# Three 256-column matmuls per weight tile on one accumulator, in place of a 512-column and a 256-column one on two halves that are added later

## The chip, the core and the metric

The kernel runs on one core of a Trainium2 chip. The metric is the device time of one execution in microseconds (us), the median of several runs. The engines that matter here are the tensor engine (PE; its weight loads are shown apart, as PEld), the vector engine (DVE), the scalar engine (ACT) and the queue that issues the loads of the weights (SP).

## What is computed

One decoder layer in float32 for 256 tokens and 2048 features: a norm; in parallel a recurrent branch (RG-LRU) and sliding-window attention; each branch is projected, gated by a sigmoid, and summed; then an output projection, norms, and an MLP with squared ReLU of 8192 features. Cut to what matters:

```python
h = rmsnorm(x, norm_mix_pre)
xr, yr, q, k, v, g_rnn, g_attn = jnp.split(h @ w_in, IN_OFFSETS, axis=-1)
xr = rg_lru(causal_depthwise_conv(xr, conv_w, conv_b), positions, w_rg_a, b_rg_a, w_rg_x, b_rg_x, lru_lambda)
y_rnn = xr * jax.nn.gelu(yr)
y_att = sliding_window_sink_attention(rope(q, positions), rope(k, positions), v, sinks)
mix = sigmoid(g_rnn) * (y_rnn @ w_rnn_proj) + sigmoid(g_attn) * (y_att @ w_attn_proj)
x = x + rmsnorm(mix @ w_out, norm_mix_post)
u = jnp.square(jax.nn.relu(rmsnorm(x, norm_mlp_pre) @ w_mlp_up))
x = x + rmsnorm(u @ w_mlp_down, norm_mlp_post)
```

## The kernel before

**The split.** Each float32 product of a projection is made of three products of reduced-precision parts. An activation x is kept as x_hi + x_lo, a weight w as w_hi + w_lo, and x·w is taken as w_hi·x_hi + w_lo·x_hi + w_hi·x_lo. Activations lie transposed in SBUF as [128 features, k tile, hi/lo, 256 tokens], so that the hi and the lo half of one k tile lie side by side, 512 columns in all. The class `Stream` loads the weights in halves of 128 × 1024 (SP queue, L67) and splits each half on the spot: ACT writes `whi` (L78), DVE writes `wlo` (L79), up to six halves ahead of their use.

**Two kinds of projection.** In `b_step` (L208 to L212) the activations are the stationary operand and the weights stream by in 512-column matmuls; keys, queries, the output projection and the second half of the MLP are made so. In `a_pair` (L179 to L198) a 128 × 128 tile of weights is stationary and the activations stream by. One call of `a_pair` makes two blocks of 128 features for the 256 tokens: 2 blocks × 16 k tiles = 32 weight tiles, in four halves of 8. It has 80 calls: 8 for the gates of the attention's projection, 16 for the two inputs of the recurrent branch (`conv` and `gelu`), 8 for the attention's projection, 8 for the gates of the recurrent branch's projection (`g_rnn`), 8 for that projection itself, and 32 for the first half of the MLP. That is 80 × 32 = 2560 weight tiles.

**One weight tile of `a_pair`.** `whi` is loaded, and one 512-column matmul (L193, `both`) passes x_hi and x_lo behind it, onto both halves of a PSUM bank; `wlo` is loaded, and one 256-column matmul (L192, for the first k tile L195) passes x_hi onto the second half of the same bank. So the bank holds w_hi·x_hi in its first half and the two small products in its second. At the end ACT copies the second halves of both blocks to SBUF (L197) and DVE adds the first halves to them (L198); the code that uses the result reads that SBUF tile.

**PSUM.** It has eight banks. A result of `a_pair` takes two of them; the pool `psa` has two such slots, and after the attention a third (`psa2`) joins them. The gates of the recurrence (`gates`, L610 to L657) have two banks of their own, `psg`. In the output projection and the MLP, `psb2` takes the four banks that `psg` and `psa2` had held.

**The gates of the recurrence.** `gates` has 256-column products of its own: for each of its weight tiles it issues `whi` with x_hi (L624), `whi` with x_lo (L625) and `wlo` with x_hi (L626), all three onto the same 256 columns of one bank, 24 matmuls in a row for each half of weights.

**What sets the order.** Each engine works through its instructions in a fixed order that the framework's scheduler chose when the program was built; an instruction that must wait holds up those behind it on its engine. Attention and the residual are generators whose stages `pump` places between the halves of the products, and some parts are pinned or given priority by hand.

Of the kernel before, what the change touches and what calls it, by code (L numbers as in the profile page):

```python
# [20 lines left out]
P = 128  # L21
# [13 lines left out]
def two_pi_parts():  # L35
    """2*pi in parts of 6 bits each, whose products with integers of up to 18 bits are exact."""
    parts, lsb, rest = [], 2.0 ** -3, TWO_PI
    for _ in range(7):
        c = float(np.floor(rest / lsb) * lsb)
        parts.append(c)  # L40
        rest -= c
        lsb *= 2.0 ** -6
    return parts


class Stream:
    """Weights in the order in which they are used: loads run ahead, and each half of a chunk is
    split into its two float32r parts ahead of the products."""
# [58 lines left out]
def layer(tc, x, pos_t, pos_row, inv_freq, vecs, sinks, gains, w_kv, w_q, w_xy, w_rg, w_g, w_rp, w_ap, w_out,  # L107
# [8 lines left out]
    psa = enter(tc.tile_pool(name="psa", bufs=2, space=bass.MemoryType.PSUM))  # L116
    pairs = [psa, psa]
# [3 lines left out]
    # ---- the weights, in the order of their use  # L121
# [32 lines left out]

    def units(name):
        return [unit(f"{name}{i}") for i in range(4)]
# [6 lines left out]
    def pump(n=1):  # L163
        """one more stage of the work that goes on beside the products"""
        for _ in range(n):
            while waiting:
                try:
                    next(waiting[0])
                    break
                except StopIteration:  # L170
                    waiting.pop(0)

    def pair(name):
        """two banks"""
        pool = pairs[0]
        pairs.append(pairs.pop(0))
        return pool.tile([P, 2, 2, S], F32, tag="pair" + pool.name, name=name)

    def a_pair(acts, out):  # L179
        """out [128 features, 2, 256 tokens] = (two column blocks of weights).T @ acts; both parts of  # L180
        the acts pass behind one load of the weights' high part"""
        ps = pair("ps")
        for f in range(2):
            both = ps[:, f].rearrange("p a b -> p (a b)")
            for half in range(2):
                hi, lo = ws.half()
                for k in range(8):
                    kt = half * 8 + k
                    a = acts[kt // 4][:, kt % 4]
                    c = slice(k * P, k * P + P)  # L190
                    if kt:
                        mm(ps[:, f, 1, :], lo[:, c], a[:, 0, :], start=False, stop=False)  # L192
                    mm(both, hi[:, c], a.rearrange("p a b -> p (a b)"), start=kt == 0, stop=kt == KT - 1)  # L193
# [3 lines left out]
        nc.scalar.copy(out, ps[:, :, 1, :])  # L197
        nc.vector.tensor_tensor(out, ps[:, :, 0, :], out, ALU.add)  # L198
# [15 lines left out]
    def b_pass512(acts, name):  # L214
        """[256 tokens, 512 columns], one bank per token block"""
# [12 lines left out]
    def transpose_split(nat, dst, tb, q, ps):  # L228
        """a quarter of nat [128 tokens, 2048 features] -> dst[q] [128 features, k tile, hi/lo, tokens]"""
# [10 lines left out]
    # ---- phase A: everything up to the merged mixers  # L240
# [37 lines left out]
    def rms(tb, k):  # L278
        """1 / sqrt(mean + eps) from the four partial sums of squares"""
# [7 lines left out]
    # ---- first norm, a token block at a time, and the keys' and values' products behind it  # L287
# [4 lines left out]
    for q in range(4):  # L292
        if q % 2 == 0:
            room = pair("gain_b")
        gain_b.append(room[:, q % 2].rearrange("p a b -> p (a b)"))
# [97 lines left out]
    # ---- rotary tables  # L393
# [25 lines left out]
    def rope(ps, tb, heads, dsts):  # L419
        """ps [128 tokens, heads * 64] -> every dst [128, heads, 64], rotated"""  # L420
# [13 lines left out]
    # ---- keys and values  # L434
# [18 lines left out]
    def attention(g, banks):  # L453
        """one group of eight heads, in stages"""
# [123 lines left out]
    # ---- recurrent branch, two blocks of 256 channels at a time  # L578
# [5 lines left out]
    def conv(n, xc):  # L584
        p3 = wide(t2("px"))
        a_pair(hT, p3)
# [13 lines left out]
    def gelu(n, th):  # L600
        py = t2("py")
        a_pair(hT, wide(py))
# [63 lines left out]
    def attn_proj(p):  # L666
        pp = t2("pp")
        a_pair(yatt, wide(pp))
        m = m1[p // 2][:, 2 * (p % 2) : 2 * (p % 2) + 2, :]
        nc.vector.scalar_tensor_tensor(m, m, 1.0, wide(pp), ALU.add, ALU.mult)  # L670
# [15 lines left out]
    # ---- the recurrent branch's projection, gated, and the merge  # L686
    def g_rnn():
        g = t2("g2")
        a_pair(hT, wide(g))
        nc.scalar.activation(g, g, AF.Tanh, scale=0.5)  # L690
        return g
# [5 lines left out]
    for p in range(8):  # L697
        pp = t2("pp")
        a_pair(yrnn, wide(pp))
# [11 lines left out]
    # ---- phase B: output projection, norms, MLP  # L711
    ctx1.close()
    pairs[:] = [psa]
# [14 lines left out]
    def b_pass1024(acts, n_kt, name, finish, n_held=HELD):  # L728
        """[256 tokens, 1024 columns]; the first token block is finished ahead of the second"""
# [17 lines left out]
    # with x1 = x + r1 * og and h2 = r2 * x1 * g2: h2 / r2 = x * g2 + r1 * (og * g2)  # L747
# [12 lines left out]
    def finish(n, tb, banks):  # L760
# [6 lines left out]
        if n == 0 and tb == 0:  # L767
            # brings the table of Sqrt in ahead of its first use
            nc.scalar.activation(st[:, 31:32], sq[:, 1, 0, 0:1], AF.Sqrt)
        if n == 1:  # L770
            if tb == 1:
                # keeps the clock of the tensor engine up over the norms
                warm = pair("warm")[:, 0, 0, 0:P]
# [6 lines left out]
            for q in range(4):  # L780
                if q % 2 == 0:
                    room = pair("ptr")
                transpose_split(h2[tb], h2T, tb, q, room[:, q % 2].rearrange("p a b -> p (a b)"))
# [19 lines left out]
    def residual():  # L803
        """x1 and r2, beside the first products of the MLP"""
# [35 lines left out]
    for f in range(2):  # L840
        uT = [unit(f"uT{f}{i}") for i in range(8)]
        def evacuate(p, u):
            nc.vector.scalar_tensor_tensor(wide(u), wide(u), 0.0, r2.unsqueeze(1).to_broadcast([P, 2, S]), ALU.max,
# [7 lines left out]
        for p in range(16):  # L851
            u = u2("u")
            a_pair(h2T, wide(u))
            full.append((p, u))
# [33 lines left out]
def lay_out(inp):  # L888
    """The arrays as the program reads them: only moved, never computed on."""
# [18 lines left out]
    # [gate, block, k, j] -> [pair of blocks, 128, block, gate, k tile, j]  # L908
# [40 lines left out]
```

## Time and profile before

| | before |
|---|---|
| measured, us | 1571.42, 1572.79, 1573.88 (median 1572.79) |
| the profiled execution: its span from first to last instruction, us (no other time of this execution is given) | 1571.5 |
| granted TensorE clock, mean | 0.997 |
| weight tiles in `a_pair` | 2560 |
| all matmuls, each with a weight load of its own | 8126 in the trace |
| DVE sums (L198) / ACT copies (L197) after `a_pair` | 80 / 80, 0.69 us / 0.58 us each |

A row of a group in the profile reads: line, engine, operation, output<-inputs by the program's names, shapes, count | busy us, mean ns of one | idle time of the engine ahead of them and who ended it. A matmul's duration runs from its start to the end of its pipeline, so neighbouring matmuls overlap in the records; what a matmul costs is the distance from its start to the next one's start. A window row reads: from:to in us, its length, the busy time with the count of instructions that touch the window, the granted clock, the share of the DMA engines' time and GB/s.

### The profile page before, as it was taken

To read this page: it belongs to the slowest core of one execution; us is meant where nothing else is said; L and a number is where in the kernel's file an instruction comes from. 1 tells how busy PE (TensorE), PEld (TensorE's weight loads), DVE (VectorE), ACT (ScalarE), POOL (GpSimd) and SP (SyncE) were. 2 spreads that over 40 slices of the span, in tenths; PEclk is the share of its full clock that TensorE was granted. 3 is DMA by queue.
4 is the path that set the end of the run, shared out by engine and by line. 5 is a ranking of instruction groups with operands and counts; after the bars stand their busy time and mean duration, and the time that the engine had idled before them with its cause. 6 is when DMAs were issued, how large, how long until landed. Compare 5 with 4: busy or idle time off the path is not lost.

```text
span 1571.5 us, 20784 instructions
## 1 busy us (share of the span) xinstructions
PE 1550.0 (99%) x8126; PEld 1306.0 (83%) x8126; DVE 975.5 (62%) x1164; ACT 804.0 (51%) x1118; POOL 1.7 (0%) x9
## 2 busy tenths in 40 slices
PE   8999999999999999999999999999999999999997
PEld 6887777788888888888787888888888888888886
DVE  6666666857758867555656756554444656554544
ACT  5545545646556775444354645444434555543432
POOL 0000000000000000000000000000000000000000
PEclk9999999999999999999999999999999999999999
DMA  6554344354655456555863555555555555555552
GB/s 247 189 169 148 128 157 149 127 186 162 209 181 194 162 187 207 183 189 185 301 212 115 200 191 181 192 190 192 193 193 187 188 190 185 189 190 196 190 197 96
DMA packets 79876, 287.85 MB, mean 183 GB/s; under 512 B 9249, under 2 KB 9505, under 8 KB 79137
## 3 DMA queue, kind: packets, MB, share of 16 engines
q1 hardware_dynamic: 79200, 285.48, 53.5%
q8 instruction: 63, 1.03, 0.2%
q10 hardware_dynamic: 578, 1.06, 0.2%
q14 instruction: 35, 0.29, 0.1%
HBM read 284.40 MB, written 2.10 MB: 182 GB/s over the span
## 4 chain that ended last, share of the span: by engine, by line
PE 95%; ACT 1%; DVE 1%; DMA 1%; issue 1%; SPq 0%; DVEq 0%
PE ps L193 38%; PE ps L192 18%; PE d L210 7%; PE d L208 7%; PE d L212 7%; PE o L208 2%; PE q L208 2%; PE o L210 2%; PE o L212 2%; PE q L210 2%; PE q L212 2%; PE sc L484 1%; PE ps L195 1%; PE po L524 1%; PE pt L516 1%
## 5 line engine op out<-in xcount | busy, mean ns | idle before, releaser
L79 DVE TENSOR_TENSOR wlo<-wraw,whi 128x1024 fp32r<-128x1024 f32 x528 | 642.7, 1223 | 430.1 <-ACT whi L78 429.1
L78 ACT CAST whi<-wraw 128x1024 fp32r<-128x1024 f32 x528 | 552.7, 1051 | 526.2 <-PE ps L193 193.9
L193 PE MATMUL ps<-hT,whi 128*128 128x512 f32 x1024 | 361.4, 398 | 0.0
L193 PE MATMUL ps<-h2T,whi 128*128 128x512 f32 x1024 | 359.0, 400 | 0.5 <-DVE h2T L237 0.5
L192 PE MATMUL ps<-hT,wlo 128*128 128x256 f32 x960 | 271.1, 282 | 0.0
L192 PE MATMUL ps<-h2T,wlo 128*128 128x256 f32 x960 | 270.7, 282 | 0.0
L193 PEld LDWEIGHTS ps<-h2T,whi 128*128 128x128 f32 x1024 | 189.4, 189 | 43.0 <-DVE h2T L237 0.9
L193 PEld LDWEIGHTS ps<-hT,whi 128*128 128x128 f32 x1024 | 189.8, 188 | 41.1 <-issue 0.7
L192 PEld LDWEIGHTS ps<-hT,wlo 128*128 128x128 f32 x960 | 181.2, 189 | 5.6 <-issue 3.1
L192 PEld LDWEIGHTS ps<-h2T,wlo 128*128 128x128 f32 x960 | 182.3, 190 | 2.6
L212 PE MATMUL d<-whi,uT 128*128 128x512 f32 x512 | 163.3, 389 | 0.0
L208 PE MATMUL d<-whi,uT 128*128 128x512 f32 x512 | 163.3, 390 | 0.0
L210 PE MATMUL d<-wlo,uT 128*128 128x512 f32 x512 | 163.3, 389 | 0.0
L208 PEld LDWEIGHTS d<-whi,uT 128*128 128x128 f32 x512 | 96.1, 188 | 20.1 <-ACT acc L870 0.3
L212 PEld LDWEIGHTS d<-whi,uT 128*128 128x128 f32 x512 | 96.1, 188 | 20.1
L210 PEld LDWEIGHTS d<-wlo,uT 128*128 128x128 f32 x512 | 96.1, 188 | 19.9
L193 PE MATMUL ps<-yrnn,whi 128*128 128x512 f32 x256 | 90.3, 398 | 0.0
L193 PE MATMUL ps<-yatt,whi 128*128 128x512 f32 x256 | 89.6, 399 | 0.0
L192 PE MATMUL ps<-yrnn,wlo 128*128 128x256 f32 x240 | 67.6, 282 | 0.7 <-ACT yrnn L656 0.7
L192 PE MATMUL ps<-yatt,wlo 128*128 128x256 f32 x240 | 67.5, 281 | 0.0
L193 PEld LDWEIGHTS ps<-yrnn,whi 128*128 128x128 f32 x256 | 47.6, 188 | 10.4
L193 PEld LDWEIGHTS ps<-yatt,whi 128*128 128x128 f32 x256 | 47.2, 188 | 10.5
(207 smaller groups left out, 1530.4 us busy)
## 6 DMA issues: line engine op xcount, KB each, us to landing
wraw<-in_w_up SPq DMA_DIRECT2D x128, 512.0 KB, 3.9
wraw<-in_w_dn SPq DMA_DIRECT2D x128, 512.0 KB, 4.0
wraw<-in_w_g SPq DMA_DIRECT2D x64, 512.0 KB, 4.5
wraw<-in_w_xy SPq DMA_DIRECT2D x64, 512.0 KB, 4.2
wraw<-in_w_q SPq DMA_DIRECT2D x32, 512.0 KB, 3.7
wraw<-in_w_ap SPq DMA_DIRECT2D x32, 512.0 KB, 4.5
wraw<-in_w_rp SPq DMA_DIRECT2D x32, 512.0 KB, 4.2
wraw<-in_w_out SPq DMA_DIRECT2D x32, 512.0 KB, 5.0
```

What stands on the lines that cost most here:

```text
L78: self.pin(self.nc.scalar.copy(hi, src))
L79: self.pin(self.nc.vector.tensor_tensor(lo, src, hi.bitcast(F32), ALU.subtract))
L192: mm(ps[:, f, 1, :], lo[:, c], a[:, 0, :], start=False, stop=False)
L193: mm(both, hi[:, c], a.rearrange("p a b -> p (a b)"), start=kt == 0, stop=kt == KT - 1)
L195: mm(ps[:, f, 1, :], lo[:, c], a[:, 0, :], start=False, stop=False)
L208: mm(banks[tb][n], a[:, 0, t], hi[:, n * 512 : n * 512 + 512], start=first, stop=False)
L210: mm(banks[tb][n], a[:, 0, t], lo[:, n * 512 : n * 512 + 512], start=False, stop=False)
L212: mm(banks[tb][n], a[:, 1, t], hi[:, n * 512 : n * 512 + 512], start=False, stop=last)
L484: mm(ps[:, i * w : i * w + w], qT[r0 : r0 + HD, h, tb * P : tb * P + P], kT[r0 : r0 + HD, g, 0:w], start=True, stop=True)
L516: nc.tensor.transpose(ps[:, h * P : h * P + P], s3[:, h % per, kb * P : kb * P + P], ident)
L524: mm(po[par * HD : par * HD + HD, :], v_sb[:, kb, g * HD : g * HD + HD], pT[par, kb], start=kb == 0, stop=kb == nk - 1)
```

## The change

`a_pair` issues three 256-column matmuls per weight tile: w_hi with x_hi, w_hi with x_lo, w_lo with x_hi, all onto the same 256 columns. Its result is half a bank per block, one bank in all, and is complete without an addition. The copy (L197) and the sum (L198) go, and the code that uses the result reads PSUM itself. `psa` has four slots of one bank; `psa2` goes; `psg` has four banks where it had two.

```diff
-    psa = enter(tc.tile_pool(name="psa", bufs=2, space=bass.MemoryType.PSUM))
-    pairs = [psa, psa]
+    psa = enter(tc.tile_pool(name="psa", bufs=4, space=bass.MemoryType.PSUM))
...
     def pair(name):
-        """two banks"""
-        pool = pairs[0]
-        pairs.append(pairs.pop(0))
-        return pool.tile([P, 2, 2, S], F32, tag="pair" + pool.name, name=name)
-
-    def a_pair(acts, out):
+        return psa.tile([P, 2, S], F32, tag="pair", name=name)
+
+    def a_pair(acts):
         ps = pair("ps")
         for f in range(2):
-            both = ps[:, f].rearrange("p a b -> p (a b)")
             for half in range(2):
                 hi, lo = ws.half()
                 for k in range(8):
                     kt = half * 8 + k
                     a = acts[kt // 4][:, kt % 4]
                     c = slice(k * P, k * P + P)
-                    if kt:
-                        mm(ps[:, f, 1, :], lo[:, c], a[:, 0, :], start=False, stop=False)
-                    mm(both, hi[:, c], a.rearrange("p a b -> p (a b)"), start=kt == 0, stop=kt == KT - 1)
-                    if kt == 0:
-                        mm(ps[:, f, 1, :], lo[:, c], a[:, 0, :], start=False, stop=False)
+                    mm(ps[:, f, :], hi[:, c], a[:, 0, :], start=kt == 0, stop=False)
+                    mm(ps[:, f, :], hi[:, c], a[:, 1, :], start=False, stop=False)
+                    mm(ps[:, f, :], lo[:, c], a[:, 0, :], start=False, stop=kt == KT - 1)
                 pump()
-        nc.scalar.copy(out, ps[:, :, 1, :])
-        nc.vector.tensor_tensor(out, ps[:, :, 0, :], out, ALU.add)
+        return ps
...
-            a_pair(hT, m)
-            nc.scalar.activation(m, m, AF.Tanh, scale=0.5)
+            nc.scalar.activation(m, a_pair(hT), AF.Tanh, scale=0.5)
...
-            psg = ctx1.enter_context(tc.tile_pool(name="psg", bufs=2, space=bass.MemoryType.PSUM))
-            pairs.append(ctx1.enter_context(tc.tile_pool(name="psa2", bufs=1, space=bass.MemoryType.PSUM)))
+            psg = ctx1.enter_context(tc.tile_pool(name="psg", bufs=4, space=bass.MemoryType.PSUM))
...
-        def evacuate(p, u):
-            nc.vector.scalar_tensor_tensor(wide(u), wide(u), 0.0, r2.unsqueeze(1).to_broadcast([P, 2, S]), ALU.max,
+        def evacuate(p, ps):
+            u = u2("u")
+            nc.vector.scalar_tensor_tensor(wide(u), ps, 0.0, r2.unsqueeze(1).to_broadcast([P, 2, S]), ALU.max,
                                            ALU.mult)
```

The other callers (`conv`, `gelu`, `attn_proj`, `g_rnn` and the merge) change in the same way: the tile that the copy and the sum had filled goes, and its reader takes the accumulator.

How the instructions stand on the tensor engine, at three places. Names: `h2T`, `yrnn` and `hT` are split activations, `ps` the accumulator, `o` the output projection's, `ptr` a bank for transposes.

First, the first weight tiles of the MLP's first half. Before:

```order
L193 MATMUL ps<-h2T_6748,whi_7263 128x512
L195 MATMUL ps<-h2T_6748,wlo_7264 128x256
L192 MATMUL ps<-h2T_6748,wlo_7264 128x256
L193 MATMUL ps<-h2T_6748,whi_7263 128x512
L192 MATMUL ps<-h2T_6748,wlo_7264 128x256
```

And with the change:

```order
L190 MATMUL ps<-h2T_8154,whi_8669 128x256
L191 MATMUL ps<-h2T_8154,whi_8669 128x256
L192 MATMUL ps<-h2T_8154,wlo_8670 128x256
L190 MATMUL ps<-h2T_8154,whi_8669 128x256
L191 MATMUL ps<-h2T_8154,whi_8669 128x256
```

Two instructions of different width have become three of one width; the accumulator's columns are the same for all three.

Second, the first call of `a_pair` on the recurrent branch's output, where it comes to the last two blocks (`yrnn_5278`, and with the change `yrnn_6243`; each has four k tiles, of which the last two come from the last block). Before:

```order
L193 MATMUL ps<-yrnn_5278,whi_5293 128x512
L192 MATMUL ps<-yrnn_5278,wlo_5294 128x256
L193 MATMUL ps<-hT_138,whi_5359 128x512
L195 MATMUL ps<-hT_138,wlo_5360 128x256
L192 MATMUL ps<-hT_138,wlo_5360 128x256
L193 MATMUL ps<-hT_138,whi_5359 128x512
L192 MATMUL ps<-hT_138,wlo_5360 128x256
L193 MATMUL ps<-yrnn_5278,whi_5293 128x512
```

And with the change:

```order
L190 MATMUL ps<-yrnn_6243,whi_6258 128x256
L191 MATMUL ps<-yrnn_6243,whi_6258 128x256
L192 MATMUL ps<-yrnn_6243,wlo_6259 128x256
L190 MATMUL ps<-yrnn_3760,whi_6288 128x256
L191 MATMUL ps<-yrnn_3760,whi_6288 128x256
```

Before, five matmuls of a later call stand between the two matmuls of the third of those four k tiles; now the call runs through without them. Ahead of this call, with the change, stand the 48 matmuls of the last gates in one row and then the 96 of one call of `a_pair`.

Third, the end of the output projection, where the first token block is transposed for the MLP while the second block's products still run. Before:

```order
L208 MATMUL o_7064<-whi_7191,mixT_5387 128x512
L233 MATMUL ptr<-ident,h_6738 128x128 x4
L210 MATMUL o_7064<-wlo_7192,mixT_5387 128x512
L212 MATMUL o_7064<-whi_7191,mixT_5387 128x512
L208 MATMUL o_7064<-whi_7209,mixT_5387 128x512
L210 MATMUL o_7064<-wlo_7210,mixT_5387 128x512
L233 MATMUL ptr<-ident,h_6738 128x128 x4
L212 MATMUL o_7064<-whi_7209,mixT_5387 128x512
```

And with the change:

```order
L204 MATMUL o_8470<-whi_8597,mixT_6382 128x512
L229 MATMUL ptr<-ident,h_8144 128x128 x4
L206 MATMUL o_8470<-wlo_8598,mixT_6382 128x512
L229 MATMUL ptr<-ident,h_8144 128x128 x4
L208 MATMUL o_8470<-whi_8597,mixT_6382 128x512
L229 MATMUL ptr<-ident,h_8144 128x128 x8
```

The groups of four transposes have moved closer together: one matmul stands between them where there were three or four, and the last group, which had stood behind the second block's products, now stands ahead of most of them.

More of the change, by code (lines that the diff above doesn't have):

```diff
@@ L292, in layer @@
     for q in range(4):
-        if q % 2 == 0:
-            room = pair("gain_b")
-        gain_b.append(room[:, q % 2].rearrange("p a b -> p (a b)"))
+        gain_b.append(narrow(pair("gain_b")))
         mm(gain_b[q], ones, gain[:, quarter(q)], start=True, stop=True)
@@ L584, in conv @@
     def conv(n, xc):
-        p3 = wide(t2("px"))
-        a_pair(hT, p3)
+        p3 = a_pair(hT)
         x3 = wide(xc)
@@ L600, in gelu @@
     def gelu(n, th):
-        py = t2("py")
-        a_pair(hT, wide(py))
+        py = narrow(a_pair(hT))
         u = t2("u")
@@ L666, in attn_proj @@
     def attn_proj(p):
-        pp = t2("pp")
-        a_pair(yatt, wide(pp))
+        pp = a_pair(yatt)
         m = m1[p // 2][:, 2 * (p % 2) : 2 * (p % 2) + 2, :]
-        nc.vector.scalar_tensor_tensor(m, m, 1.0, wide(pp), ALU.add, ALU.mult)
+        nc.vector.scalar_tensor_tensor(m, m, 1.0, pp, ALU.add, ALU.mult)
     for m in range(4):
@@ L688, in g_rnn @@
         g = t2("g2")
-        a_pair(hT, wide(g))
-        nc.scalar.activation(g, g, AF.Tanh, scale=0.5)
+        nc.scalar.activation(g, narrow(a_pair(hT)), AF.Tanh, scale=0.5)
         return g
@@ L697, in layer @@
     for p in range(8):
-        pp = t2("pp")
-        a_pair(yrnn, wide(pp))
+        pp = narrow(a_pair(yrnn))
         g = ahead.pop(0)
@@ L712, in layer @@
     ctx1.close()
-    pairs[:] = [psa]
     ctx2 = ExitStack()
@@ L771, in finish @@
             if tb == 1:
-                warm = pair("warm")[:, 0, 0, 0:P]
+                warm = pair("warm")[:, 0, 0:P]
                 for i in range(WARM_NORM):
@@ L780, in finish @@
             for q in range(4):
-                if q % 2 == 0:
-                    room = pair("ptr")
-                transpose_split(h2[tb], h2T, tb, q, room[:, q % 2].rearrange("p a b -> p (a b)"))
+                transpose_split(h2[tb], h2T, tb, q, narrow(pair("ptr")))
         for i in range(2):
@@ L851, in layer @@
         for p in range(16):
-            u = u2("u")
-            a_pair(h2T, wide(u))
-            full.append((p, u))
+            full.append((p, a_pair(h2T)))
             if f == 0 and p == R2_AT:
```

2 lines of the change are left out of this document (added).

## Prediction

> **What bounds the kernel now.** I read the page's busy times first, then the chain that ended last.
>
> ```profile
> span 1571.5 us, 20784 instructions
> PE 1550.0 (99%) x8126; PEld 1306.0 (83%) x8126; DVE 975.5 (62%) x1164; ACT 804.0 (51%) x1118; POOL 1.7 (0%) x9
> PE 95%; ACT 1%; DVE 1%; DMA 1%; issue 1%; SPq 0%; DVEq 0%
> ```
>
> The tensor engine is busy for 99% of the span and makes up 95% of the chain. Work spared on DVE or ACT cannot show in the time unless the tensor engine waits for it; what counts is the distance from one matmul's start to the next one's. The groups of the tensor engine, shapes kept apart, say how often the changed piece runs:
>
> ```profile
> L193 PE MATMUL ps<-hT,whi 128*128 128x512 f32 x1024 | 361.4, 398 | 0.0
> L193 PE MATMUL ps<-h2T,whi 128*128 128x512 f32 x1024 | 359.0, 400 | 0.5 <-DVE h2T L237 0.5
> L193 PE MATMUL ps<-yrnn,whi 128*128 128x512 f32 x256 | 90.3, 398 | 0.0
> L193 PE MATMUL ps<-yatt,whi 128*128 128x512 f32 x256 | 89.6, 399 | 0.0
> ```
>
> One such matmul per weight tile: 1024 + 1024 + 256 + 256 = 2560 tiles, with hardly any idle time ahead of them. So each nanosecond per tile is 2.56 us. The mean durations are no price, since neighbours overlap; the price comes from windows of the tensor engine that begin and end at starts of matmuls:
>
> ```profile
> core 0: us, PE busy (x), PEclk, DMA share, GB/s
> 512.93:515.66 2.73, 2.73 (x26) 1.00 0.57 197
> ...
> 575.21:577.95 2.74, 2.74 (x26) 1.00 0.58 190
> 578.25:581.10 2.85, 2.85 (x26) 1.00 0.54 180
> 1033.31:1207.62 174.31, 174.31 (x770) 1.00 0.55 187
> 1207.62:1388.31 180.69, 180.69 (x1025) 1.00 0.57 192
> ```
>
> The last row is the first half of the MLP in its second round: 16 calls of `a_pair`, 16 x 32 = 512 weight tiles, 1024 matmuls (a count in a row takes in those that reach into the window). The row above it is `b_step`, 768 matmuls of 512 columns. The first row is one half of weights in `gates`: 24 matmuls of 256 columns, **the very pattern that the change brings**: the same weights twice, then the low part, all three onto the same 256 columns. The timeline shows it beside one tile of `a_pair`:
>
> ```profile
> 1300.08 0.28 PE L192 MATMUL ps<-h2T,wlo 128*128 128x256 f32 x1
> 1300.19 0.40 PE L193 MATMUL ps<-h2T,whi 128*128 128x512 f32 x1
> 1300.43 0.28 PE L192 MATMUL ps<-h2T,wlo 128*128 128x256 f32 x1
> ```
>
> ```profile
> 513.28 0.28 PE L624 MATMUL pg<-xs,whi 128*128 128x256 f32 x1
> 513.39 0.28 PE L625 MATMUL pg<-xs,whi 128*128 128x256 f32 x1
> 513.50 0.28 PE L626 MATMUL pg<-xs,wlo 128*128 128x256 f32 x1
> 513.62 0.28 PE L624 MATMUL pg<-xs,whi 128*128 128x256 f32 x1
> ```
>
> 0.35 us per tile there, 0.34 us here.
>
> **The change, part by part.** *The stream of matmuls.* Before: 180.69 us / 512 = 352.9 ns per tile. With the change: 2.73 us / 24 = 113.8 ns per matmul, times three 341.3 ns (the second `gates` row gives 2.74 / 24, so 342.5). The tile passes 768 columns either way. Where all are of one width the price goes by the column: 174.31 us / 768 = 227.0 ns for 512, twice the 113.5 of a 256. So the 12 ns that `a_pair` pays on top look like the price of alternating widths, and go with it. Saved: 352.9 − 341.3 = 11.6 ns x 2560 = **29.7 us**. The 2560 additional weight loads are within this price, since each `gates` matmul has a load of its own too; what this term rests on is that a pattern seen in runs of 24 and 48 holds for thousands.
>
> Here a rule of the Trainium skill speaks against the change: TensorE: Matmul & The Clock Gate, section Back-to-back issue gap, gives a warm matmul its columns at 2.4 GHz and 2.5 ns on top, whatever the width. By it one matmul more costs 2.5 ns x 2560 = 6.4 us, an estimate from that page, and the sum would end above the time before. The trace disagrees: 113.5 and 227.0 ns are one to two, which leaves no room for such a part.
>
> *Copies and sums.* 80 ACT copies (L197) and 80 DVE sums (L198) go, of 0.58 and 0.69 us each; 32 of them are
>
> ```profile
> L197 ACT COPY u<-ps 128x512 f32<-128x512 f32 x32 | 18.7, 584 | 53.5 <-PE ps L193 53.5
> L198 DVE TENSOR_TENSOR u<-ps,u 128x512 f32<-128x512 f32 x32 | 22.1, 691 | 34.2 <-ACT u L197 34.2
> ```
>
> They lie beside the products, and where nobody waits that is worth nothing. The waits list of the tensor engine names where somebody does:
>
> ```profile
> PE ptr L233 <- DVE h L779: 1.5, 2, 1.2
> PE o L208 <- DVE pp L198: 1.4, 1, 1.4
> ...
> PE ps L192 <- ACT yrnn L656: 0.7, 1, 0.7
> ```
>
> The second row is the start of the output projection: `psb2` takes the banks of `psa2`, and the last sum still reads them. With the change its banks come from `psg`, done 170 us earlier. **1.4 us saved**; next in line are weights that are split far ahead, so nothing replaces it.
>
> *Four banks for `gates`.* The view of line L624 has under idle time:
>
> ```profile
>   ACT room L629: 1.0, 5
> ```
>
> The gates wait for one of their two banks. With four, each call has a bank for each of its four results. **1.0 us saved.**
>
> *The order at the last recurrent block.* Before, products of `hT` fill the time until `yrnn` of the last block is split; with the change fewer stand there. The split was late already:
>
> ```profile
> 597.88 0.39 PE L192 MATMUL ps<-yrnn,wlo 128*128 128x256 f32 x1 [0.72 <-ACT yrnn L656]
> 598.23 0.68 DVE L657 TENSOR_TENSOR yrnn<-xct,yrnn 128x512 fp32r<-128x512 f32 x1
> ```
>
> The gates end at 581.10 (window row above), the low part is there at 598.91, 17.8 us later. With the change the tensor engine comes to it after 96 matmuls and 14 tiles: 96 x 113.8 ns + 14 x 341.3 ns = 15.7 us. It waits for up to 2.1 us in place of 0.7. With four banks the second run of 24 need not start 0.30 us after the first one's end (577.95 to 578.25 in the window rows), so the chain may start that much earlier; I take a wait of 1.7: **1.0 us lost** (between 0.7 gained, with no wait left, and 1.4 lost).
>
> *The transposes at the norms* stand closer together. Four transposes wait for a DVE step of 0.69 us (four in 2.74 us); with one matmul of 0.23 us between, up to some 0.3 us each may be lost, against a last group that no longer stands behind the products. The wait there is 1.5 us in all (first row of the list), so I take 0, between 1 us lost and 1 us gained.
>
> ```profile
> 836.68 2.74 DVE L779 SCALAR_TENSOR_TENSOR h<-h,st,xg 128x512 f32<-128x512 f32 x4
> ```
>
> *Accumulators held longer.* Their readers now hold PSUM itself. With four slots a result has three calls' time, 3 x 32 x 341.3 ns = 32.8 us, until its slot is wanted. The longest hold is at the start of the MLP, where three results wait for `r2`; its matmuls stand at the end of the third call:
>
> ```profile
> 886.13 0.60 PE L833 MATMUL pr<-dg,ones 128*128 128x128 f32 x4
> ```
>
> The fifth call wants the first slot some 11 us after that, and the first reader is one DVE step. Cost 0; if a hold broke this cover, each microsecond would count in full.
>
> *Feeding.* Each half of weights is used up in 2.73 us, where it was 2.82, and ACT and DVE must split it in that time.
>
> ```profile
> 435.00:640.00 205.00, 204.28 (x1206) 178.81 (x1205) 152.73 (x189) 133.92 (x188) 0.00 (x0) 1.00 0.56 186
> ```
>
> In the stage that loads DVE most (columns: PE, PEld, DVE, ACT) it is busy for 152.73 of 205 us, ahead of the 0.69 us per call that it is spared. Cost 0.
>
> **The sum.** 29.7 + 1.4 + 1.0 − 1.0 = 31.1 us off the profiled span of 1571.5: 1540.4. The median measured, 1572.79, lies 1.3 us above that span: **1541.7 us**, 2.0% faster.
>
> **Rivals.** *A fixed price per matmul (slower).* The 12 ns may belong not to the alternation but to each short matmul in `a_pair`. If a 512 costs 227.0 there too, the 256 costs 352.9 − 227.0 = 125.9 ns, three 377.7 ns, 24.8 ns more than before: 1572.8 + 63.5 − 1.4 = 1634.9 us. A milder form of it is the stretch of `gates` at 578.25: 2.85 / 24 x 3 = 356.3 ns, 3.4 more, 1572.8 + 8.7 − 1.4 = 1580.1. It decides from 352.9 / 3 = 117.6 ns per matmul on; the clean `gates` rows, with the same kind of operands, are 4 ns below that, and the longer ones hold waits for a bank. Chance 0.09 together, the rule of the skill among them.
>
> *The 12 ns stay for another reason* (how `whi` and `wlo` reach the array while DVE and ACT write the next ones): then a tile still costs 352.9 ns and only the 1.4 us go: 1571.4 us. Against it: the split goes on beside `gates` too. Chance 0.05.
>
> *Half of the gain is given back*, to loads that come late in long runs (192 GB/s in the last window row would become 199) or to attention, whose chains have 3% less cover: some 15 us less, 1557. The stage above with its 25% of idle DVE speaks against it. Chance 0.10.
>
> That the change doesn't do what it says is out: the order shows three matmuls per tile.
>
> **How the numbers follow.** The forecast has 0.76: its tile costs between 339 ns (113.0 per matmul, the four rows of the timeline) and 345 ns, which gives 1535 to 1552 with the small terms. With the case of half the gain the range is 1533 to 1560, some 0.83. Within 0.2% (3.1 us, about what a measurement of this kernel can tell from no change) are 1569.7 to 1575.9: 0.05. Slower 0.09, faster 0.86.
>
> **What would show it.** Right: in the first half of the MLP, second round, 512 tiles in 174.7 us, starts 0.11 us apart in all three lines; `psa2`'s wait of 1.4 us gone; a wait of 1 to 2 us for `yrnn`; DVE 80 x 0.69 = 55 us less busy, ACT 80 x 0.58 = 46 us less. Wrong: starts over 117.6 ns apart, or idle time ahead of `ps` that names `whi` or `wlo`.

## The result, and the profile after

The changed kernel takes 1584.82 us (median of four runs, 1584.35 to 1586.00), the kernel before beside it 1572.11 us. The ratio is 1.0081, with a 95% interval of 1.0069 to 1.0093. The forecast of 1541.7 us, 2% faster, was wrong, sign included: the change costs 0.8%.

The page of the changed kernel: span, busy times, the shares of the chain that ended last, and three groups of the tensor engine (PEld rows are weight loads).

```profile
span 1584.2 us, 25803 instructions
PE 1566.4 (99%) x10686; PEld 1442.6 (91%) x10686; DVE 927.3 (59%) x1084; ACT 764.7 (48%) x1038; POOL 1.7 (0%) x9
PE 96%; DMA 1%; ACT 1%; DVE 1%; issue 1%; SPq 0%; DVEq 0%; ACTq 0%
L190 PE MATMUL ps<-h2T,whi 128*128 128x256 f32 x1024 | 290.0, 283 | 0.0
L190 PEld LDWEIGHTS ps<-h2T,whi 128*128 128x128 f32 x1024 | 196.6, 192 | 0.2
L206 PEld LDWEIGHTS d<-wlo,uT 128*128 128x128 f32 x512 | 96.1, 188 | 19.9
```

The tensor engine bounds the kernel as before, and has no idle time ahead of the new matmuls. DVE and ACT were relieved (975.5 to 927.3 us and 804.0 to 764.7 us busy; 48.2 and 39.3 us less, where 55 and 46 were forecast), which is worth nothing by itself. So the loss must lie in the distance from start to start. The timeline of the changed kernel (start, duration, engine, line) in the first half of the MLP:

```profile
1299.73 0.28 PE L190 MATMUL ps<-h2T,whi 128*128 128x256 f32 x1
1299.85 0.28 PE L191 MATMUL ps<-h2T,whi 128*128 128x256 f32 x1
1299.97 0.28 PE L192 MATMUL ps<-h2T,wlo 128*128 128x256 f32 x1
1300.09 0.28 PE L190 MATMUL ps<-h2T,whi 128*128 128x256 f32 x1
```

Three starts take 0.36 us, where the four `gates` rows of the prediction took 0.34. Windows of the tensor engine in the changed kernel price it. The rows are one call of `gates` (48 matmuls), the output projection with the norms behind it, the end of that stretch alone, `b_step` in the MLP (768 matmuls of 512 columns), and 512 tiles of `a_pair` (1536 matmuls):

```profile
core 0: us, PE busy (x), PEclk, DMA share, GB/s
469.21:474.67 5.46, 5.46 (x51) 1.00 0.58 187
763.16:858.10 94.94, 93.41 (x430) 1.00 0.60 205
852.24:858.10 5.86, 4.36 (x30) 1.00 0.00 0
1042.95:1217.30 174.35, 174.35 (x771) 1.00 0.62 187
1217.30:1401.61 184.31, 184.31 (x1538) 1.00 0.63 189
```

In `a_pair` 184.31 / 1536 = **120.0 ns** per matmul, 360.0 ns per tile. In `gates`, in the same run, 5.46 / 48 = **113.7 ns** for the same pattern. `b_step` is unchanged at 174.35 / 768 = 227.0 ns. For the kernel before, the second and third of these stretches read

```profile
752.67:850.41 97.74, 94.26 (x429) 0.99 0.56 198
841.30:850.41 9.11, 5.63 (x35) 0.84 0.00 0
```

The waits of the tensor engine in the changed kernel (us in total, times, longest) no longer have a row for the first matmul of the output projection; two of its rows:

```profile
PE ps L191 <- DVE yrnn L648: 0.7, 1, 0.7
PE ptr L229 <- DVE h L765: 0.6, 1, 0.6
```

The books close. A tile costs 360.0 − 352.9 = 7.1 ns more, times 2560 is +18.2 us. The output projection with its norms takes 2.8 us less, the wait of 1.4 us ahead of it is gone, and the four calls of `gates` take 4 × 5.46 = 21.84 us. Before, they took 23.60 us, of which three matmuls of `a_pair` that stood among them, two wide and one narrow, are 0.59 us by the price of a tile there (1.67 × 352.9 ns): 1.2 us less. The sum is +12.8 us; the spans differ by 1584.2 − 1571.5 = 12.7.

So one question was left: why does the same instruction, in the same pattern, cost 113.7 ns in `gates` and 120.0 ns in `a_pair`?

### The profile page after: what moved, and what is told of

Its sections match the earlier page's. It is cut to its first block, busy times and chain, and to the rows that moved or that the text cites. A ratio compares the mean times of both kernels' runs of the same rounds, so it can differ in the third digit from the quotient of the medians.

```text
span 1584.2 us, 25803 instructions
## 1 busy us (share of the span) xinstructions
PE 1566.4 (99%) x10686; PEld 1442.6 (91%) x10686; DVE 927.3 (59%) x1084; ACT 764.7 (48%) x1038; POOL 1.7 (0%) x9
## 4 chain that ended last, share of the span: by engine, by line
PE 96%; DMA 1%; ACT 1%; DVE 1%; issue 1%; SPq 0%; DVEq 0%; ACTq 0%
PE ps L190 19%; PE ps L191 19%; PE ps L192 19%; PE d L204 7%; PE d L206 7%; PE d L208 7%; PE o L204 2%; PE o L208 2%; PE o L206 2%; PE q L204 2%; PE q L206 2%; PE q L208 2%; PE sc L478 1%; PE po L518 1%; PE pt L510 1%
## 5 line engine op out<-in xcount | busy, mean ns | idle before, releaser
L190 PE MATMUL ps<-hT,whi 128*128 128x256 f32 x1024 | 291.8, 285 | 0.0
L191 PE MATMUL ps<-hT,whi 128*128 128x256 f32 x1024 | 290.5, 284 | 0.0
L192 PE MATMUL ps<-hT,wlo 128*128 128x256 f32 x1024 | 290.2, 283 | 0.0
L190 PE MATMUL ps<-h2T,whi 128*128 128x256 f32 x1024 | 290.0, 283 | 0.0
L192 PE MATMUL ps<-h2T,wlo 128*128 128x256 f32 x1024 | 289.8, 283 | 0.0
L191 PE MATMUL ps<-h2T,whi 128*128 128x256 f32 x1024 | 289.8, 283 | 0.0
L192 PEld LDWEIGHTS ps<-hT,wlo 128*128 128x128 f32 x1024 | 196.4, 192 | 2.8 <-issue 2.8
L190 PEld LDWEIGHTS ps<-hT,whi 128*128 128x128 f32 x1024 | 196.4, 192 | 2.0 <-issue 1.3
L191 PEld LDWEIGHTS ps<-hT,whi 128*128 128x128 f32 x1024 | 196.4, 192 | 1.5 <-issue 1.3
L190 PEld LDWEIGHTS ps<-h2T,whi 128*128 128x128 f32 x1024 | 196.6, 192 | 0.2
L191 PEld LDWEIGHTS ps<-h2T,whi 128*128 128x128 f32 x1024 | 196.6, 192 | 0.0
L192 PEld LDWEIGHTS ps<-h2T,wlo 128*128 128x128 f32 x1024 | 196.6, 192 | 0.0
L191 PE MATMUL ps<-yrnn,whi 128*128 128x256 f32 x256 | 72.6, 283 | 0.7 <-DVE yrnn L648 0.7
L190 PE MATMUL ps<-yrnn,whi 128*128 128x256 f32 x256 | 72.6, 283 | 0.0
```

What stands on the lines that cost most here:

```text
L190: mm(ps[:, f, :], hi[:, c], a[:, 0, :], start=kt == 0, stop=False)
L191: mm(ps[:, f, :], hi[:, c], a[:, 1, :], start=False, stop=False)
L192: mm(ps[:, f, :], lo[:, c], a[:, 0, :], start=False, stop=kt == KT - 1)
```

## The experiments

The theory I went in with is PLACE. In the memory layout of the built program, the activations that `a_pair` streams (`hT`, `yatt`, `yrnn`, `h2T`) and the weights `whi` and `wlo` all begin at byte 416 of a partition, modulo 1024; `xs`, which `gates` streams, begins at 96. PLACE says that a matmul's pitch depends on where its two operands lie. The rivals: REGION (it matters in which part of SBUF, or how far apart, the pools are), RUN (how long matmuls accumulate onto the same columns), and RATE (a long stretch runs at a slower pace, whatever lies where). All times of a single run stand beside one run of the kernel before on the same chip: 1571.02 us for the first four, 1572.98 for the next three. Addresses below are modulo 1024.

**1. Weights 192 bytes further on** (`w192`). `xs`, laid out behind the weights, moves as well.

```diff
     big = enter(tc.tile_pool(name="big", bufs=12))
+    padp = enter(tc.tile_pool(name="pad", bufs=1))
+    nc.gpsimd.memset(padp.tile([P, 48], F32, name="pad"), 0.0)
     wpool = enter(tc.tile_pool(name="w", bufs=2))
```

> The changed kernel with 192 bytes per partition left free ahead of the pool of the weights, so that whi and wlo (and what lies behind them, xs among it) move by 192 bytes against the activations in big. Theory PLACE (a weight load slows the stream where weights and moving activations lie at the same address modulo 1024 or a smaller power of two; now both at 416, in the recurrent gates 416 against 96): the three matmuls of a tile start 113.5 ns apart in place of 120.0, a tile costs 341 ns in place of 360, total about 1535 us. Theories REGION (the activations' end of SBUF is slower to stream from), RUN (48 matmuls in a row onto the same columns) and RATE (instructions can't be issued faster): 120.0 ns, total about 1584 us.

Measured: 1583.75 us. The same three stretches as above (`gates`, `b_step`, 512 tiles of `a_pair`) in this run:

```profile
467.00:472.65 5.65, 5.65 (x51) 1.00 0.62 181
1034.13:1213.38 179.25, 179.25 (x771) 1.00 0.60 182
1213.38:1394.28 180.90, 180.90 (x1538) 1.00 0.64 192
```

Per matmul 117.7 ns in `gates`, 233.4 in `b_step`, 117.8 in `a_pair`. The 113.5 ns that PLACE hoped for did not come, so as a forecast this missed. But all three prices moved, with nothing changed except addresses (`whi` and `wlo` now begin at 608, `xs` at 288), and what `a_pair` won `b_step` lost.

**2. The pools in the other order** (`swap`).

```diff
-    big = enter(tc.tile_pool(name="big", bufs=12))
     wpool = enter(tc.tile_pool(name="w", bufs=2))
+    big = enter(tc.tile_pool(name="big", bufs=12))
```

> The changed kernel with the pools of weights and of activations in swapped order: weights at 2 to 66 KB of each partition, activations at 66 to 163 KB; all of them still at 416 modulo 1024. REGION: the starts come closer together, towards 113.5 ns, total towards 1535 us. PLACE, RUN and RATE: 120.0 ns, total about 1584 us.

Measured: 1584.74 us, with `gates` at 5.46 us, `b_step` at 174.32 and the 512 tiles at 184.32: 113.7, 227.0 and 120.0 ns, as before the swap. REGION is out.

**3. Only `xs` moved**, from 96 to 416 (`xs320`).

```diff
     rnn = {}
+    nc.gpsimd.memset(pa.tile([P, 80], F32, name="pad"), 0.0)
```

> The changed kernel with the moving operand of the recurrent gates, xs, shifted by 320 bytes, from 96 to 416 modulo 1024, the place of the weights; everything else stays. PLACE: the matmuls of the gates start 120.0 ns apart in place of 113.7, the total grows by 1.2 us (192 matmuls by 6.3 ns), no more than noise. REGION, RUN and RATE: the gates stay at 113.7 ns.

Measured: 1585.94 us. The same stretches:

```profile
468.48:474.24 5.76, 5.76 (x51) 1.00 0.58 182
1042.90:1217.22 174.32, 174.32 (x771) 1.00 0.61 187
1217.22:1401.53 184.31, 184.31 (x1537) 1.00 0.63 189
```

`gates` goes from 5.46 to 5.76 us: 5.76 / 48 = **120.0 ns**, exactly the price of `a_pair`, and all four calls of `gates` take 5.76 us; the rest stays. The records of the weight loads in `gates` grow with it, from 188 to 192 ns in the mean, as long as those of `a_pair`, though the weights did not move. This is the clean proof: the price that the prediction took from `gates` was the price of the address of `xs`.

**4. Short accumulations** (`short_runs`): six matmuls onto one block's columns, then six onto the other's, each run started afresh, so that most of the sum over k tiles is left out.

```diff
-                    mm(ps[:, f, :], hi[:, c], a[:, 0, :], start=kt == 0, stop=False)
+                    mm(ps[:, kt // 2 % 2, :], hi[:, c], a[:, 0, :], start=kt % 2 == 0, stop=False)
...
-                    mm(ps[:, f, :], lo[:, c], a[:, 0, :], start=False, stop=kt == KT - 1)
+                    mm(ps[:, kt // 2 % 2, :], lo[:, c], a[:, 0, :], start=False, stop=kt % 2 == 1)
```

> The changed kernel with the accumulation of a_pair cut into runs like those of the recurrent gates: six matmuls onto one block's 256 columns, then six onto the other's, each run started afresh (so most of the sum over k tiles is left out). RUN: starts 113.5 ns apart, total about 1535 us. PLACE, REGION and RATE: 120.0 ns, total about 1584 us.

Measured: 1585.12 us; 5.46 us for a call of `gates` and 184.32 us for the 512 tiles, again 120.0 ns. RUN is out. RATE is out with experiment 3, where a run of 48 matmuls paid 120.0 as well.

**5 to 7. Every buffer at an address of its own.** Gaps behind each buffer let one run show many pairs of addresses: 32 bytes behind every weight half and every activation unit (`step32`), 64 bytes behind the weight halves alone (`stepw64`), 64 bytes behind the activation units alone (`stepb64`).

```diff
-            hi = self.pool.tile([P, 1024], F32R, tag="whi", bufs=WHALF, name=f"whi{j}")
+            hi = self.pool.tile([P, 1032], F32R, tag="whi", bufs=WHALF, name=f"whi{j}")[:, 0:1024]
...
-        return big.tile([P, 4, 2, S], dt, tag="U8", name=name)
+        return big.tile([P, 2056], dt, tag="U8", name=name)[:, 0:2048].rearrange("p (a b c) -> p a b c", a=4, b=2)
```

(`step32`; 1040 in the first line and its like for `wlo` makes `stepw64`, 2064 in the second alone makes `stepb64`.)

> The changed kernel with 32 bytes left free behind each buffer of whi, wlo and of the activations, so that the buffers of each kind lie at six (activations: twelve) different places modulo 256. PLACE: the starts are no longer 120.0 ns apart throughout but take values from 113 to 120 by the buffers in use, changing from one half of weights to the next; the total lies between 1535 and 1584 us. If only the difference of the two addresses counts, cells of the same difference have the same distance. RATE and REGION: 120.0 ns everywhere, 1584 us.

> The changed kernel with 64 bytes left free behind each buffer of whi and wlo only; the activations stay at 416 modulo 1024. PLACE: distances between starts change with the buffer of the weights in use, with a period of at most four buffers (256 bytes). Total between 1535 and 1584 us. RATE and REGION: 120.0 ns, 1584 us.

> The changed kernel with 64 bytes left free behind each buffer of the activations only; all weights stay at one place. PLACE: distances change with the buffer of the activations, every four k tiles. Total between 1535 and 1584 us. RATE and REGION: 120.0 ns, 1584 us.

Measured: 1584.28, 1583.33 and 1583.19 us. The means over the 512 tiles are 118.1, 118.2 and 118.8 ns per matmul, and `b_step` costs 232.2, 230.9 and 231.7 ns. The totals say little; the stretches inside do. In `stepb64` each activation unit serves 12 matmuls in a row. Five such windows, the first three with `yatt`, the last two with `h2T`:

```profile
331.29:332.66 1.37, 1.37 (x14) 1.00 0.75 275
332.66:334.02 1.36, 1.36 (x14) 1.00 0.41 75
334.02:335.44 1.42, 1.42 (x14) 1.00 0.81 294
1216.47:1217.88 1.41, 1.41 (x14) 1.00 1.00 285
1219.31:1220.75 1.44, 1.44 (x14) 1.00 1.04 361
```

That is 114, 113, 118, 118 and 120 ns (a window's end is known to 0.01 us, so to 1 ns per matmul). The units of the five rows begin at 864, 96, 416, 864 and 416; all weights begin at 160. The same figures come back with nearly every return of a unit. Away from the breaks by other matmuls, units at 608 and at 96, modulo 512 both 96, stand at 113 to 115 ns, and those at 416 and 928, modulo 512 both 416, at 118 to 120. But the first and the fourth row have the same two addresses and differ by 3 ns: the unit at 864 costs 114 behind one at 32 and 118 behind one at 736. So the pair of addresses counts, and it does not settle the price alone; what the stream did just before counts too. In `stepw64` the activations stay put and only the weights' buffers differ:

```profile
1222.46:1223.86 1.40, 1.40 (x15) 1.00 0.88 319
1223.86:1225.22 1.36, 1.36 (x15) 1.00 0.30 99
1225.22:1226.65 1.43, 1.43 (x15) 1.00 0.90 284
1230.93:1232.37 1.44, 1.44 (x14) 1.00 0.63 148
```

113 to 120 ns. (The first two rows are one half of weights; there the stream takes six starts at 118 ns and then goes on at 113.) So the addresses of both operands count, each by itself. `step32` missed what was hoped of it: activations and weights moved in equal steps, and its stretches of one unit and one half of weights still differ, from 117.3 to 119.8 ns in the MLP's second round. One number for the distance between the operands does not give the price: `h2T` units at 416 and at 576, each 448 bytes (modulo 1024) from the low part of its weights, cost 118.2 and 119.8 ns.

**8 to 10. The kernel with the operands where `gates` has them**, activations at 96 and weights at 416, for the changed kernel (`like_gates`) and for the one before (`before_like`); and the gaps of `step32` in the kernel before (`before_step32`).

```diff
     const = enter(tc.tile_pool(name="const", bufs=1))
+    nc.gpsimd.memset(enter(tc.tile_pool(name="pad", bufs=1)).tile([P, 48], F32, name="pad"), 0.0)
     big = enter(tc.tile_pool(name="big", bufs=12))
+    nc.gpsimd.memset(enter(tc.tile_pool(name="pad2", bufs=1)).tile([P, 80], F32, name="pad2"), 0.0)
     wpool = enter(tc.tile_pool(name="w", bufs=2))
+    const2 = enter(tc.tile_pool(name="const2", bufs=1))
...
-    ones = const.tile([P, P], F32, name="ones")
+    ones = const2.tile([P, P], F32, name="ones")
```

> The changed kernel with all activations moved down by 320 bytes, from 416 to 96 modulo 1024; the weights stay where they are, at 416. So a_pair's moving and stationary operands lie to each other as those of the recurrent gates did. PLACE: starts 113.6 ns apart, a tile 341 ns, 49 us less; b_step, which now has its weights at 416 against activations at 96, goes from 227 to 230 to 233 ns per matmul, 7 to 14 us more; total 1540 to 1550 us, faster than before. A fixed price per weight load or per matmul, whatever the place: 120.0 ns, 1584 us.

> The kernel before with the same shift of the activations by 320 bytes. If only loads that meet the stream at a bad place cost time (PLACE), a tile costs 227 + 113.6 = 341 ns here too, 31 us less, and b_step 7 to 14 us more: 1548 to 1558 us, and against the changed kernel at the same place it is at most some us slower (the waits that the change takes away). If alternating widths has a price of its own, as the prediction had it, the tile stays at 353 ns: 1579 to 1587 us.

> The kernel before with 32 bytes left free behind each buffer of weights and activations, so that all places occur. PLACE: the even 352.9 ns per tile break up, by the buffers in use, around 350 ns in the mean, and b_step goes from 227 to some 232 ns: total 1575 to 1585 us. Price of widths or of loads alone: 352.9 ns throughout, 1572 us.

Measured, with the kernel before at 1571.42 us (median of 8): `like_gates` 1550.56 us, ratio **0.986 (0.9845 to 0.9876)**; `before_like` 1577.31 us, ratio 1.004 (1.0026 to 1.0054), 19 us above the range that PLACE had for it; `before_step32` 1577.95 us in a single run. In `like_gates`, a stretch of 240 matmuls at the start of the MLP's first half, the rest of its first round (1248 matmuls), `b_step`, and the 512 tiles of the second round:

```profile
833.57:860.76 27.19, 27.19 (x242) 1.00 0.75 238
865.21:1012.28 147.07, 147.07 (x1252) 1.00 0.63 189
1012.28:1189.87 177.59, 177.59 (x770) 1.00 0.60 184
1189.87:1363.97 174.10, 174.10 (x1537) 1.00 0.66 199
```

And in `before_like` its `b_step` and its 512 tiles (1024 matmuls):

```profile
1033.53:1209.46 175.93, 175.93 (x770) 1.00 0.57 186
1209.46:1389.93 180.47, 180.47 (x1026) 1.00 0.57 192
```

At this place a tile costs 174.10 / 512 = **340.0 ns** with the change and 180.47 / 512 = **352.5 ns** without it: 12.5 ns saved, where the prediction said 11.6, and the order of the two kernels turns round, 1550.56 to 1577.31 us. That the 12 ns are a price of alternating widths is not shown by this, and two things speak against it. The first round of the same execution of `like_gates` ran at 147.07 / 1248 = 117.8 ns per matmul, 353.5 ns per tile, no less than the old pattern, without any change of width. And `before_step32`, where a tile costs 178.56 / 512 = 348.7 ns in the mean, has stretches of the old pattern, four tiles each, at 352 and at 342 ns. Three of them, all with the same `yatt` unit, the last two with the same weight buffers, the first with others:

```profile
339.53:340.94 1.41, 1.41 (x10) 1.00 0.62 212
345.13:346.50 1.37, 1.37 (x10) 1.00 0.50 173
361.90:363.27 1.37, 1.37 (x10) 1.00 0.81 248
```

With widths of 512 and 256 by turns, 1.37 / 4 = 342 ns per tile is what the prediction gave to three narrow matmuls (341.3, or 342.5 by its second row of `gates`). So the old pattern too has more than one price, and its 352 ns may be the slower pace of the new pattern (353.5) as well as a price of widths.

The windows of `like_gates` show two more things. `b_step` pays for the move, 177.59 / 768 = 231.2 ns for 227.0 (228.9 in its second round). And the same matmuls, on the same activations, cost 27.19 / 240 = 113.3 ns up to one moment and 147.07 / 1248 = 117.8 ns from there to the end of the round. The timeline at that moment:

```profile
864.62 0.28 PE L194 MATMUL ps<-h2T,whi 128*128 128x256 f32 x1
864.73 0.28 PE L195 MATMUL ps<-h2T,wlo 128*128 128x256 f32 x1
864.85 0.60 PE L820 MATMUL pr<-dg,ones 128*128 128x128 f32 x4
865.21 0.36 PE L193 MATMUL ps<-h2T,whi 128*128 128x256 f32 x1
865.41 0.28 PE L194 MATMUL ps<-h2T,whi 128*128 128x256 f32 x1
865.53 0.28 PE L195 MATMUL ps<-h2T,wlo 128*128 128x256 f32 x1
```

Four small matmuls break the stream, and it resumes at the slower pace. A break can also lead the other way. Early in the same execution 48 matmuls on `hT` run at 5.66 / 48 = 117.9 ns; then come four transposes of attention (`pq`), and from the sixth matmul behind them 19 run at 2.15 / 19 = 113.2:

```profile
144.62:150.28 5.66, 5.66 (x50) 1.00 0.62 182
151.30:153.45 2.15, 2.15 (x21) 1.00 0.54 204
```

**11 and 12. Other places.** Activations at 608 and weights at 160, the best pair of `stepb64` (`place608`); and the same with `mixT` and `uT`, the stationary operands of `b_step`, 64 bytes further on, so that they and the weights lie alike modulo 512, as they did before (`two_places`).

```diff
+    nc.gpsimd.memset(enter(tc.tile_pool(name="pad", bufs=1)).tile([P, 48], F32, name="pad"), 0.0)
     big = enter(tc.tile_pool(name="big", bufs=12))
+    nc.gpsimd.memset(enter(tc.tile_pool(name="pad2", bufs=1)).tile([P, 144], F32, name="pad2"), 0.0)
     wpool = enter(tc.tile_pool(name="w", bufs=2))
```

and for `two_places` beside it (with fewer `T2` and `u2` buffers to make room; every activation buffer is 512 bytes longer, so that the units stand at 608 and at 96 by turns)

```diff
-        return big.tile([P, 4, 2, S], dt, tag="U8", name=name)
+        at = 16 if name.startswith(("uT", "mixT")) else 0
+        t = big.tile([P, 2176], dt, tag="U8", name=name)
+        return t[:, at : at + 2048].rearrange("p (a b c) -> p a b c", a=4, b=2)
```

> The changed kernel with the activations at 608 and the weights at 160 modulo 1024, the pair of places that gave 113.4 ns in all of its 55 stretches in the run with the activations' buffers stepped by 64 bytes (the last run, at 96 and 416, kept 113.3 ns except in the MLP's first round, where it ran at 117.8 ns after the two small matmuls for r2). If the pair of places alone decides: 113.3 to 113.6 ns throughout, first round of the MLP included, total about 1545 us. If the moment at which a stretch begins decides as well: some stretches at 117 to 118 ns again, total 1545 to 1555 us. A fixed price per load: 120.0 ns, 1584 us.

> As the run before it, and the activations that are stationary in b_step (mixT, uT) lie 64 bytes further on, at the weights' own place modulo 512, where b_step took 227 ns; to make room for it, two scratch pools are smaller (T2 5, u2 2). PLACE: a_pair 113.4 ns, b_step of the output projection and of the MLP 227 ns in place of 231, some 8 us less than the run before it: about 1537 us, faster than both kernels. If scratch becomes short, idle time appears ahead of ps or of the attention's transposes.

Measured, with the kernel before at 1572.05 us: `place608` 1558.76 us (five runs, 1549.76 to 1559.56), ratio 0.9919 (0.9901 to 0.9937); `two_places` **1547.85 us** (five runs), ratio **0.9846 (0.9828 to 0.9864)**, the best kernel of the study beside `like_gates`, whose interval overlaps it. Both miss what was expected of them, 1545 to 1555 and 1537 us. Four runs of `two_places` took 1546.76 to 1548.42 us, the fifth, which is the profiled one, 1562.43. Its `b_step` and its 512 tiles:

```profile
1022.55:1196.89 174.34, 174.34 (x771) 1.00 0.62 187
1196.89:1377.79 180.90, 180.90 (x1537) 1.00 0.63 192
```

`b_step` is back at 227.0 ns, as hoped. The tiles stand at 180.90 / 1536 = 117.8 ns in this one execution. In the profiled execution of `place608` (1549.76 us) the second round costs 113.3 ns and the first, again from the four small matmuls on, 117.8. One layout thus has two paces, and in `like_gates`, `place608` and `two_places` a stretch keeps its pace until other matmuls or a wait break it. The four shorter executions of `two_places` have no trace, so their pace is not shown.

## Why the prediction was wrong

**What bounds the kernel** was right: the tensor engine, by the distance of starts.

**The stream** is the step that failed. It put 341.3 ns on a tile and saved 29.7 us; the tile costs 360.0 ns and the stream lost 18.2, which is 47.9 of the miss. What failed first was the price: 113.8 ns was measured on `xs` and charged to activations at another address, where the same pattern costs 120.0. Where the operands lie as in `gates` the forecast saving does come (12.5 ns per tile), but only at the faster of two paces; at the slower one a tile costs 353.5 ns and nothing is saved. What failed beside it was the reason given for the 12 ns, the alternating widths: the old pattern, widths alternating, ran at 342 ns per tile in stretches of `before_step32`. The prediction saw that something was carried over and put its doubt on the wrong thing, that the pattern "holds for thousands"; length has nothing to do with it, as the 48 matmuls at 120.0 ns in experiment 3 show. The phrase that hid the error stands at the rival, "with the same kind of operands": the same kind, not the same place.

**The rival on the other side** had the right criterion, 117.6 ns per matmul; 120.0 lies above it, and its milder form, 1580.1 us, came nearest. Its mechanism did not hold: no fixed price belongs to a short matmul, since 256 columns cost 113.3 ns at another address, half of the 227.0 that 512 columns cost in `b_step`. These two numbers, each from the best place measured, leave no room for the 2.5 ns on top of each matmul that the Trainium skill gives (TensorE: Matmul & The Clock Gate, section Back-to-back issue gap); the page gives it for an isolated warm matmul, so it was not made for a stream like this one. The rival by which the 12 ns stay had the time wrong, 352.9 ns per tile for 360.0, but was right in that they need not belong to the alternation. That half of the gain is given back to loads or attention did not happen: no idle time ahead of `ps` names a weight.

**The small terms**, against the profiled span. The wait for `psa2`'s banks, 1.4 us, went, as forecast. `gates` with four banks: 1.2 us won for 1.0. The wait for `yrnn`: 0.7 us as before, where 1.7 was forecast, so the 1.0 lost was not lost; with tiles of 360.0 ns for 341.3 the tensor engine comes to it later. The norm at the output projection was put at 0 and won 2.8 us. It lies behind the last `o` matmul: 9.11 us there before, at a granted clock of 0.84, and 5.86 us now at 1.00, less some 0.4 us that the transposes now cost ahead of it. Most of it is waits. The prediction counted the 1.5 us of the list's first row, and two rows of the same list stand for the same norm:

```profile
PE ptr L233 <- DVE h2T L237: 0.6, 1, 0.6
PE ps L193 <- DVE h2T L237: 0.5, 1, 0.5
```

The three are 2.6 us before, and one wait of 0.6 is left. The other 1.3 us are time in which the engine is busy (5.63 us before, 4.36 now): four transposes fewer stand there, and the clock is higher; how it divides between the two is not shown. Copies, sums, longer holds and the feeding cost nothing, as forecast; `gates` and the tiles ran without a wait for a bank or a weight.

Sum of the misses: 47.9 − 0.2 − 1.0 − 2.8 = 43.9 us; the spans differ from the forecast by 1584.2 − 1540.4 = 43.8.

**Shown, and not shown.** That the addresses of the operands change the price is shown: by moving the streamed operand alone (`xs320`, `stepb64`), the weights alone (`stepw64`), and by the whole kernel turning from 0.8% slower to 1.4% or 1.5% faster with padding. That they alone set it is not so: one pair of addresses had two paces in `stepb64`, `like_gates` and `place608`. That the streaming operand and the loads of the next weights get in each other's way when both are read fits the load records, 192 ns where the pace is 120.0 and 188 in `b_step` and in the `gates` of the changed kernel, but no view shows the reads themselves. What sets the pace in which a stretch begins stays open; the traces show breaks that change it either way, and no run was made to try one. Whether the old pattern's 352 ns are such a slower pace stays open as well.

## What to carry to other kernels

A price per matmul read from one place of a kernel holds for another place only if both operands lie alike, and even then it can be one of two; compare their addresses in a partition before carrying it over, as well as their shapes. When a pattern of matmuls comes out slower than its twin with no wait in front of it, a pad of some hundred bytes between the pools of the streamed and the stationary operand is a cheap trial: here two of the pads were worth 34 and 37 us of 1585, and 192 bytes at one place (`w192`) 1 us. The projections that share a buffer pull its address in different directions (what freed `a_pair` cost `b_step` 2 to 6 ns per matmul), so each pair of operands is priced apart.

## What the runs showed of the hardware

The same 256-column matmul with its weight load, at a granted clock of 1.00 and with no wait recorded, ran in long stretches at 113.3, 117.8 and 120.0 ns, and a 512-column one at 227.0 to 233.4 ns, by the addresses of its two operands and, at one layout, by the pace in which a stretch began. With both at 416 the 256-column stream kept the slowest of these three (120.0) in four kernels, and for `b_step`'s 512 columns the same place was the best (227.0). The Trainium skill, page "TensorE: Matmul & The Clock Gate", section "Step-by-step: what each phase is for", says that loading the next tile's weights "doesn't steal SBUF read bandwidth from the running matmul". As a general rule this is hard to square with the runs, where the pitch changes from 113 to 120 ns with the weights' address alone (`stepw64`); the reads themselves no run shows.

At one layout the stream has two paces, 113.3 and 117.8 ns. In `like_gates` a break by four small matmuls moved it from the first to the second, where it stayed for 1248 matmuls; earlier in the same execution four transposes had moved it from the second to the first. Executions of one kernel differed by 15 us at a granted clock of 1.00 (`two_places`, 1547 and 1562 us); that the two paces make this difference fits and is not shown, since only the longest execution has a trace.
